# Decoder step on one core: how the attention deals out its eight PSUM banks

## The chip, the cores and the metric

The kernel runs as one program on one core of a Trainium2 chip. The metric is device time in microseconds (us) of one launch, lower is better. The core has a matmul engine (TensorE, PE in the profile, its weight loads PEld), VectorE (DVE), ScalarE (ACT), GpSimd (POOL), queues for DMA, a working memory (SBUF) and a small memory into which alone the matmul engine writes (PSUM). PSUM is used here as eight banks of 128 partitions by 512 fp32 values; a matmul's output lies in one bank, and VectorE or ScalarE copy it out (an eviction) before the bank is written again.

## The reference

One step of a decoder trunk with two layers, for 512 new prompt positions and 8 sequences with 4 new sample positions each, 544 columns in all, width 1024, fp32:

```python
for i in range(DEPTH):                     # 2 layers
    x = x + 0.5 * swiglu(rmsnorm(x, norm_ffn1[i]), w_ffn1_in[i], w_ffn1_out[i])
    h = rmsnorm(x, norm_mix[i])
    if i % 2 == 0:                         # dilated windows (128,1), (512,4), (2048,16)
        m = dilated_mixer(h, caches, w_qkv_a, w_out_a)
    else:                                  # chunked spatial gating
        m = chunk_gmlp(h, w_uv_b, ln_g, ln_b, w_s, b_s, w_out_b)
    x = x + m
    x = x + 0.5 * swiglu(rmsnorm(x, norm_ffn2[i]), w_ffn2_in[i], w_ffn2_out[i])
y = rmsnorm(x, norm_final)
```

In the mixer of layer 0, q, k and v of three groups (8 heads of 64 each) come from one projection. The prompt attends within itself, the sample positions attend to cached keys and values and to themselves; the three groups are merged by their softmax denominators and projected by `w_out_a`. The outputs are `y` and the new rows of the caches.

## The kernel before

**Products.** Weights stand still, the 544 columns of activations stream past in two halves of 272. Each fp32 matrix is split into a high and a low part (`split`, L234: ScalarE casts `wh`, VectorE subtracts `wl`), and a product runs three passes per 128 rows of the contraction (`passes`, L243, matmuls at L247): `wh` with the activations' high part, `wh` with their low part, `wl` with the high part. `plain` (L262) makes four results from one load of weights, two column blocks by two halves; each takes one bank `z`, accumulates 24 matmuls in it (8 blocks of 128 by three passes) and is then evicted by `take`, in the attention at a raised priority (`soon`, L134).

**The attention** (L752) works on pairs of heads, `hp` 0 to 3. `UNITS` (L31) is the program order of one pair, a prime marks work for the pair before:

```python
UNITS = "U1 AV' BV' b K1 B1 U2 rk1 K2 B2 A12 U0 E12 rk2 K0 B0 A0 D U3 E0 rk0 M v0 v1 U4 v2"
```

`U0` to `U4` are products that make q, k or v of a group; VectorE's eviction writes `qT`, `kT`, `vT` (L231). What begins with A, E, M, v and `rk` is the prompt's: scores (L864 and L895 into banks `sm`, masked by VectorE), exponentials, merge, and the values (L974): per block ScalarE scales the scores, PE transposes four blocks into a bank (L989, L1003), ScalarE copies them to `pt` (L991, L1005), and four matmuls add to the sum `ya` or `yb` (L994, L1008), each a bank held until the last block (L1010, L1011). What begins with b, B, K, D is the sample's, in banks `sb`: rows of q, k and v are transposed (L1027), q goes out to `q_rows` and comes back spread over the partitions as `qb` by DMA, POOL multiplies it with cached keys into `prod`, VectorE reduces that to scores `sc` (L1132); `decide` (L1149) makes the softmax; the values (L1179) add up in one bank `yo` from L1213 over L1216 to the copy at L1220, with POOL's products and VectorE's reductions (L1194) between.

At the end of the attention the output projection runs in two parts (L830, L836), each a contraction of 256, so that one result is six matmuls; its eviction adds to `x` (L410), which has been read back from `x_away`. The first part and all of the above lie between `heads(True)` (L781) and `heads(False)` (L833), that is, with `few` set.

**Banks and order.** `bank` (L108) deals out the banks by tags: tag "m" has four, "n" and "o" have two each. Outside the attention products rotate in "m" (`z`) and "n" (`z2`), small matmuls in "o". With `few` set, products take "n", the prompt's small matmuls "m", the sample's "o". A planner orders each engine's instructions when the program is built: by priority, which is program order unless raised, among what its own estimate of times says is ready, and a tile that finds none of its tag's buffers free waits for one. On the chip each engine then follows that order; semaphores make it wait for data and for banks. Only products of the first unit (before L781) run in the attention without `few`.

Of the kernel before, what the change touches and what calls it, by code (L numbers as in the profile page):

```python
# [94 lines left out]
class Ctx:  # L95
# [11 lines left out]

    def bank(self, kind):  # L108

        few = {"z": "n", "sm": "m", "sb": "o"}  # L110
        tag = (few if self.few else {"z": "m", "z2": "n", "sm": "o"})[kind]
        return self.pp.tile([P, 512], F32, tag=tag, name=f"ps_{kind}", bufs=4 if tag == "m" else 2)

    def heads(self, on):
# [1372 lines left out]
```

## Time and profile before

| | us |
|---|---|
| median of 3 runs | 2368.95 |
| lowest, highest | 2368.46, 2370.94 |
| the profiled execution | 2366.76 |
| its span, first to last instruction | 2365.0 |
| busy: PE, PEld | 2322.5, 2282.1 |
| busy: DVE, ACT, POOL | 1781.5, 1137.9, 117.5 |

The profile is of one execution. Busy time is the time in which an engine had an instruction in work; matmuls overlap each other in it. POOL works in the attention alone, from about 416 to 766 us of the span. A group of the profile is named by line, engine, operation and tiles, `ps_z` for a product's bank, `ps_sm` and `ps_sb` for those of the prompt's and the sample's small matmuls. "Idle before" is the time that the engine stood still ahead of an instruction, with what ended it. The granted clock is TensorE's, 1.00 at full speed.

### The profile page before, as it was taken

The numbers are of one execution on the slowest core, as the hardware profiler recorded it, in microseconds if no ns is written. First come the engines' busy times: TensorE is split into PE (matmuls) and PEld (weight loads), VectorE is DVE, ScalarE is ACT, GpSimd is POOL, SyncE is SP. The second block draws the span as 40 slices with busy tenths as digits, with TensorE's granted clock in tenths as the row PEclk, the third lists the DMA queues.
The fourth block names the chain that finished last, engine by engine and source line by source line (L and its number), as shares of the span: only waits on it lengthen the run. The fifth ranks groups of instructions, "written<-read, shape, count | busy, mean of one in ns | idle before, by whom it ended". The sixth has DMA issues, their size and how long they took to land.

```text
span 2365.0 us, 44134 instructions
## 1 busy us (share of the span) xinstructions
PE 2322.5 (98%) x18316; PEld 2282.1 (96%) x18316; DVE 1781.5 (75%) x3011; ACT 1137.9 (48%) x1879; POOL 117.5 (5%) x100
## 2 busy tenths in 40 slices
PE   8999999999999999999999999999999999999997
PEld 8999999989898999999999999999999999999997
DVE  8878585656656978768887858799977778878583
ACT  7444354444435734435644424666644536435253
POOL 0000000342332000000000000000000000000000
PEclk9999999999999999999999999999999999999999
DMA  4323235565554332323232323334433322223231
GB/s 148 107 90 108 75 124 161 137 179 163 146 159 118 119 108 90 108 77 120 72 107 86 112 72 118 99 129 143 138 112 115 101 90 90 90 90 123 74 117 39
DMA packets 308000, 263.40 MB, mean 111 GB/s; under 512 B 7352, under 2 KB 303384, under 8 KB 307800
## 3 DMA queue, kind: packets, MB, share of 16 engines
q1 hardware_dynamic: 284104, 242.88, 33.0%
q10 hardware_dynamic: 23696, 17.70, 2.6%
q8 instruction: 144, 2.36, 0.4%
q14 instruction: 56, 0.46, 0.1%
HBM read 243.78 MB, written 16.78 MB: 110 GB/s over the span
## 4 chain that ended last, share of the span: by engine, by line
PE 89%; DMA 4%; DVE 2%; POOL 1%; issue 1%; ACT 1%; ACTq 0%; POOLq 0%; DVEq 0%; SPq 0%
PE ps_z L247 84%; POOL prod L231 1%; DMA other<-in_cache_kv_w_dram 1%; DMA q_rows<-sn 1%; DMA qb<-q_rows 1%; PE ps_sm L1361 1%; PE ps_sm L1290 0%; ACT wh L238 0%; DVE wl L231 0%; PE ps_sm L864 0%; PE ps_sb L1213 0%; PE ps_sb L1117 0%; PE ps_sm L1363 0%; PE ps_z L685 0%; DVE s L231 0%
## 5 line engine op out<-in xcount | busy, mean ns | idle before, releaser
L247 PE MATMUL ps_z<-xbh,wh 128*128 128x272 f32 x2164 | 629.6, 294 | 6.9 <-DVE x L410 2.3
L247 PE MATMUL ps_z<-xbl,wh 128*128 128x272 f32 x2164 | 625.3, 290 | 0.0
L238 ACT CAST wh<-raw 128x1024 fp32r<-128x1024 f32 (+3 forms) x404 | 355.3, 881 | 553.2 <-PE ps_z L247 528.6
L247 PE MATMUL ps_z<-xbh,wl 128*128 128x272 f32 x2164 | 620.4, 290 | 0.0
L247 PE MATMUL ps_z<-abh,wl 128*128 128x272 f32 x1792 | 516.3, 290 | 0.0
L247 PE MATMUL ps_z<-abl,wh 128*128 128x272 f32 x1792 | 513.8, 288 | 0.0
L247 PE MATMUL ps_z<-abh,wh 128*128 128x272 f32 x1792 | 512.3, 288 | 0.3 <-ACT abh L204 0.3
L247 PE MATMUL ps_z<-th,wh 128*128 128x272 f32 x1648 | 477.1, 290 | 5.1 <-DVE f L375 2.7
L247 PE MATMUL ps_z<-th,wl 128*128 128x272 f32 x1648 | 477.6, 290 | 0.0
L247 PE MATMUL ps_z<-tl,wh 128*128 128x272 f32 x1648 | 476.3, 290 | 0.4 <-DVE tl L231 0.4
L231 DVE TENSOR_TENSOR wl<-raw,wh 128x1024 fp32r<-128x1024 f32 (+3 forms) x404 | 411.2, 1021 | 54.4 <-ACT wh L238 52.5
L247 PEld LDWEIGHTS ps_z<-xbh,wh 128*128 128x128 f32 x2164 | 407.2, 189 | 15.7 <-issue 4.1
L247 PEld LDWEIGHTS ps_z<-xbl,wh 128*128 128x128 f32 x2164 | 409.7, 189 | 1.9 <-issue 0.8
L247 PEld LDWEIGHTS ps_z<-xbh,wl 128*128 128x128 f32 x2164 | 406.5, 189 | 2.2 <-issue 1.5
L238 ACT CAST wh<-s 128x1024 fp32r<-128x1024 f32 x206 | 216.4, 1050 | 257.1 <-PE ps_z L247 251.6
L247 PEld LDWEIGHTS ps_z<-abl,wh 128*128 128x128 f32 x1792 | 337.4, 189 | 0.1
L247 PEld LDWEIGHTS ps_z<-abh,wl 128*128 128x128 f32 x1792 | 336.6, 188 | 0.2
L247 PEld LDWEIGHTS ps_z<-abh,wh 128*128 128x128 f32 x1792 | 335.3, 188 | 0.6 <-ACT abh L204 0.5
L247 PEld LDWEIGHTS ps_z<-th,wh 128*128 128x128 f32 x1648 | 311.3, 189 | 6.4 <-DVE f L375 3.2
L247 PEld LDWEIGHTS ps_z<-tl,wh 128*128 128x128 f32 x1648 | 311.1, 189 | 0.9 <-DVE tl L231 0.6
L247 PEld LDWEIGHTS ps_z<-th,wl 128*128 128x128 f32 x1648 | 311.2, 189 | 0.3
L231 DVE TENSOR_TENSOR wl<-s,wh 128x1024 fp32r<-128x1024 f32 x206 | 251.3, 1220 | 33.2 <-ACT wh L238 33.0
(275 smaller groups left out, 2427.4 us busy)
## 6 DMA issues: line engine op xcount, KB each, us to landing
raw<-in_w_ffn_in_dram SPq DMA_DIRECT2D x88, 1024.0 KB, 5.1
raw<-in_w_ffn_out_dram SPq DMA_DIRECT2D x32, 1024.0 KB, 5.2
raw<-in_w_uv_b_dram SPq DMA_DIRECT2D x24, 1024.0 KB, 5.3
raw<-in_w_qkv_a_dram SPq DMA_DIRECT2D x36, 512.0 KB, 5.2
other<-in_cache_kv_w_dram SPq DMA_DIRECT2D x28, 512.0 KB, 4.8
raw<-in_w_ffn_out_dram SPq DMA_DIRECT2D x16, 768.0 KB, 4.4
raw<-in_w_out_b_dram SPq DMA_DIRECT2D x16, 768.0 KB, 4.4
other<-in_cache_kv_w_dram SPq DMA_DIRECT2D x28, 256.0 KB, 3.5
```

Source lines behind the costliest of these rows:

```text
L231: eng.tensor_tensor(out, a, b, op=op)
L238: g.nc.scalar.copy(t[0], a)
L247: g.nc.tensor.matmul(z, a, b, start=(first and s == 0), stop=(last and s == 2), skip_group_check=True)
L1361: nc.tensor.matmul(pm[:, n * P:(n + 1) * P], vn[:, n, iss], wst[:, gq], start=True, stop=True)
```

## The change

With `few` set, a product now takes its bank from the tags "n" and "o" in turn, two banks each, so four in rotation. The small matmuls of prompt (`sm`) and sample (`sb`) both take tag "m", four banks together, where they had four and two. Outside the attention nothing changes. `turn` is set to False by `heads` and was used before only in `banks`, which no product between L781 and L833 calls.

```diff
     def bank(self, kind):
 
-        few = {"z": "n", "sm": "m", "sb": "o"}
-        tag = (few if self.few else {"z": "m", "z2": "n", "sm": "o"})[kind]
+        if self.few:
+
+            self.turn = not self.turn if kind == "z" else self.turn
+            tag = "m" if kind != "z" else "no"[self.turn]
+        else:
+            tag = {"z": "m", "z2": "n", "sm": "o"}[kind]
         return self.pp.tile([P, 512], F32, tag=tag, name=f"ps_{kind}", bufs=4 if tag == "m" else 2)
```

## The prediction

> **What bounds the kernel now.** I read the page first: span, busy time of the engines, costliest groups.
>
> ```profile
> span 2365.0 us, 44134 instructions
> ...
> L247 PE MATMUL ps_z<-xbh,wh 128*128 128x272 f32 x2164 | 629.6, 294 | 6.9 <-DVE x L410 2.3
> ```
>
> The products (L247, `ps_z`) are the big groups and they hardly wait: 6.9 us of idle time in front of this one. The matmul engine sets the time, and only its gaps can be had. The change acts on the attention alone, so I cut that stage into windows (columns: PE, PEld, DVE, ACT, POOL busy, granted clock, DMA).
>
> ```profile
> 416.00:476.00 60.00, 58.83 (x447) 53.96 (x446) 38.72 (x100) 24.96 (x66) 20.77 (x12) 1.00 0.53 141
> ...
> 716.00:766.00 50.00, 47.06 (x350) 42.57 (x349) 36.24 (x74) 25.94 (x72) 13.93 (x16) 0.90 0.41 121
> sum 350.00, PE 335.78 PEld 309.52 DVE 221.22 ACT 148.58 POOL 117.27; mean PE 55.96 PEld 51.59 DVE 36.87 ACT 24.76 POOL 19.54
> ```
>
> ```profile
> 830.00:890.00 60.00, 60.00 (x479) 60.00 (x478) 42.64 (x66) 22.70 (x29) 0.00 (x0) 1.00 0.33 106
> ```
>
> Of 350 us PE is busy 335.78: 14.2 us idle, 0.6% of the span, is the most that any order of the same work could win here, apart from the half-clock stretches below. The window of the FFN in the second fence has no gap at all. What ends the gaps is in the waits of PE in the stage (what waits, for whom, us in total, times, longest):
>
> ```profile
> PE ps_sm L864 <- DVE kT L231: 3.6, 2, 2.9
> PE ps_z L247 <- DVE x L410: 2.3, 3, 1.6
> PE ps_sb L1027 <- DVE kT L231: 2.1, 2, 1.1
> PE ps_z L247 <- DVE kT L231: 2.1, 2, 1.8
> PE ps_sb L1213 <- DVE ssum L1209: 1.3, 1, 1.3
> PE ps_sb L1113 <- DMA other<-in_cache_kv_w_dram: 0.8, 1, 0.8
> PE ps_z L247 <- DVE qT L231: 0.8, 1, 0.8
> ```
>
> Two kinds must be kept apart. A product that waits for DVE's write of `kT`, `qT` or `x` reads none of these: it waits for the bank which that eviction empties. These **bank waits** are 2.3 + 2.1 + 0.8 = 5.2 us. A small matmul that waits for `kT` (L864, the scores; L1027, a transpose) or for `ssum` (L1213) reads that very tile: these **data waits** are 3.6 + 2.1 + 1.3 = 7.0 us. The longest of each, DVE's rows ahead of PE's (the timeline: start, us, what, in brackets the idle time before and what ended it):
>
> ```profile
> 594.45 1.22 DVE L1132 TENSOR_REDUCE sc<-prod 128x16 f32<-128x1024 f32 x1 [3.38 <-POOL prod L231]
> 595.58 0.68 DVE L1011 TENSOR_TENSOR y<-y,ps_sm 128x512 f32<-128x512 f32 x1
> 596.78 1.22 DVE L1132 TENSOR_REDUCE sc<-prod 128x16 f32<-128x1024 f32 x1 [0.53 <-POOL prod L231]
> 597.92 0.62 DVE L231 TENSOR_TENSOR kT<-ps_z,rstd 128x272 f32<-128x272 f32 x1
> ```
>
> ```profile
> 596.13 0.71 PE L895 MATMUL ps_sm<-kT,qT 64*128 64x128 f32 x6
> 598.60 0.39 PE L247 MATMUL ps_z<-xbh,wh 128*128 128x272 f32 x1 [1.75 <-DVE kT L231]
> ```
>
> ```profile
> 532.00 0.43 DVE L231 TENSOR_TENSOR kT<-ps_z,rstd 128x272 f32<-128x272 f32 x1
> ```
>
> ```profile
> 528.23 0.28 PE L247 MATMUL ps_z<-xbh,wh 128*128 128x272 f32 x1
> 528.35 0.29 PE L247 MATMUL ps_z<-xbl,wh 128*128 128x272 f32 x1
> ...
> 528.98 0.60 PE L963 MATMUL ps_sm<-cst,kT 128*128 128x128 f32 x4
> 532.48 0.49 PE L864 MATMUL ps_sm<-kT,qT 64*128 64x128 f32 x4 [2.91 <-DVE kT L231]
> ```
>
> The reader is to see the same cause twice: DVE takes its queue in order, the eviction of `kT` stands behind reductions of the sample's scores (L1132), and these wait for POOL. PE then stands still, once for the bank and once for the data.
>
> **The change part by part.** No instruction is added or removed; banks are dealt out differently, and the planner orders PE's work anew by its own estimate of when banks come free.
>
> *Products: two banks become four.* Products start 0.12 to 0.13 us apart (528.23, 528.35), so a half of 24 matmuls takes 3.0 us. With two banks PE may run one half ahead of the eviction; with four, three. Two more halves are 6.0 us of cover against a longest bank wait of 1.8 us; in the output projection a half has six matmuls, 0.75 us, so two more cover 1.5 of the 1.6 us. The 5.2 us of bank waits therefore go almost whole, as waits.
>
> What is late next is the data. DVE still works its queue at POOL's pace: before the wait at 598.60 it idles 3.38 and 0.53 us for POOL, and four banks hurry neither. PE runs ahead, then meets the next small matmul whose tile DVE has not written. Below, nothing is given back (5.2 us won), above, everything (0 won). I take half, 2.6 us, since bank and data waits are of like size and stand beside each other in the same stretches. The planner may also put the next unit's products into the hole between the last eviction and the scores (528.98 to 532.48), which two banks forbade: from 0 to the 7.0 us of data waits; I take 0.5 us, since what made that wait long is POOL's lateness, and the planner that set this order did not see it.
>
> *Small matmuls: four banks and two become four in all.* This adds waits. Who holds banks long is seen in one head's values:
>
> ```profile
> 572.58 0.44 PE L994 MATMUL ps_sm<-pt,spare 128*64 128x128 f32 x4
> ...
> 574.82 1.44 PE L1213 MATMUL ps_sb<-ssum,cache 128*128 128x64 f32 x11
> ...
> 583.09 0.66 PE L1008 MATMUL ps_sm<-pt,spare 128*64 128x128 f32 x8
> ```
>
> ```profile
> 582.65 0.59 ACT L1010 COPY y<-ps_sm 128x512 f32<-128x512 f32 x1 [1.38 <-PE ps_sm L994]
> 584.38 1.07 ACT L1005 COPY pt<-ps_sm 128x512 f32<-128x512 f32 x2 [1.14 <-PE ps_sm L1003]
> 585.62 0.43 ACT L1220 COPY y<-ps_sb 64x32 f32<-64x32 f32 x2 [0.16 <-PE ps_sb L1216]
> ```
>
> The prompt's first sum `ya` is written from 572.58 and copied out at 582.65, ten microseconds; the sample's sum `yo` from 574.82 to 585.62, eleven; the second sum `yb` from 583.09 until DVE reads it at 595.58 (L1011 above), twelve. So of four shared banks two are bound for most of it, and two are left for the transposes and for the next head's sample rows, where four were left before, three of the prompt's and one of the sample's. Two suffice to alternate, since a step is four transposes (L989 or L1003), a copy by ACT of about 0.53 us (1.07 for two) and four matmuls. A transposing matmul that finds no bank stops everything behind it on PE, products included, until ACT's copy lands.
>
> The price: below zero is possible, as longer runs of one kind save switches; a first product behind small ones comes 0.23 us before the next (598.60 to 598.83 in the same timeline) and not 0.125, so a switch costs about 0.1 us. Above, all eight steps of four heads wait for a copy: 32 × 0.53 = 17 us. Three heads have the next head's products to lay between, and there a bank short of one is a different order and some more switches: 0.1 us × 8 × 3, at half, 1.2 us. The last head has almost no products left, but its eight steps were alternating already; I put nothing there. I take 1 us in all, near the lower end, by the switch, because the rows show ACT waiting for PE at every copy (1.38, 1.14), and not the other way round.
>
> ```profile
> 598.83 0.29 PE L247 MATMUL ps_z<-xbl,wh 128*128 128x272 f32 x1
> ```
>
> *The clock.* Three stretches of the stage ran at half the granted clock:
>
> ```profile
> 492.08:495.49 3.41, 3.41 (x24) 2.75 (x20) 3.31 (x5) 1.65 (x4) 2.36 (x4) 0.50 0.89 259
> 533.05:536.46 3.41, 3.41 (x16) 3.41 (x17) 3.29 (x8) 0.22 (x1) 0.00 (x0) 0.50 0.75 217
> 737.85:748.08 10.23, 10.23 (x48) 9.68 (x46) 9.15 (x10) 5.32 (x14) 5.85 (x7) 0.50 0.82 232
> ```
>
> 17.05 us at half clock cost up to 8.5 us. The second follows the data wait at 532.48, the others stretches of small matmuls. Since the longest data wait stays, I expect them to stay: 0, with bounds of one stretch fewer or more, 3.41/2 = 1.7 us each way. [...]
>
> **The sum.** −2.6 − 0.5 + 1 + 0 = −2.1 us. The profiled execution spans 2365.0 us and took 2366.76 us, 2.2 us under the median of 2368.95 us; I apply the difference to the median: 2368.95 − 2.1 ≈ **2366.8 us**. A change under 0.2%, 4.7 us, can't be told from none here.
>
> **The rivals.**
> - *PE really runs ahead* (faster): the bank waits go whole (−5.2), the new order closes half of the data waits (−3.5), and the stretch behind 532.48 keeps its clock (−1.7), against +1 for the shared banks: −9.4, 2359.5 us. For it: PE is the bound, and each gap stands beside products that only a bank held back. Against it: DVE's idle time for POOL is unchanged.
> - *Small matmuls wait for banks* (slower): the place is the values of a head, above all of the last, where no product covers. If two sums and `yo` hold three banks and transposes are left with one, each step waits for ACT's copy. The last head alone: 8 × 0.53 = 4.2; four steps each of the other three: 12 × 0.53 = 6.4; one more half-clock stretch 1.7; less the 2.6 won: +9.7, 2378.7 us. It decides the sign from about seven exposed copies on (7 × 0.53 = 3.7, against 3.1 won), and is slower by over 0.2% from about fifteen. For it: the three sums are held 10 to 12 us each. Against it: `yo` and `yb` overlap for 2.5 us only (583.09 to 585.62).
> [...]
> - *It does not do what it says*: the planner orders as before and PE stalls a few us later for the same DVE rows; 2369 us.
>
> **How the numbers follow.** Forecast, about 2 us won: 0.40. Does nothing: 0.07. Faster, 2359.5: 0.31. Shared banks, slower, 2378.7: 0.19. Clock: 0.03. Those within 0.2% give 0.47; faster 0.31; slower 0.22, the clock's rival counted as slower. The likeliest alone lies in 2364.2 to 2368.9. The range reaches past the faster case, to 2358, and into the slower one, to 2377, where the price of 17 us above makes its end uncertain: left out are about half of the slower case and the far end of the faster, some 0.15.
>
> **What would show it.** In PE's waits of the attention the rows `ps_z L247 <- DVE x, kT, qT` shrink from 5.2 to under 1.5 us. L864 and L1027 waiting for `kT` keep or grow beyond 5.7 us: then half is given back. If `ps_sm` or `ps_sb` rows waiting for ACT copies (`pt`, `sn`, `kt`) come to microseconds, the shared banks bite, first of all after 737. PE's idle time in 416 to 766 should be 11 to 13 us in place of 14.2, and the half-clock time about 17 us. The prediction is wrong if the new order of PE, which no row of this profile can show, moves the sample's transposes (L1027) by microseconds: they start the chain over DMA and POOL on which DVE waits.

## The result, and the profile after

| | before | after |
|---|---|---|
| median of 3 runs, us | 2368.95 | 2410.85 |
| lowest, highest | 2368.46, 2370.94 | 2408.77, 2411.03 |
| span of the profiled execution, us | 2365.0 | 2406.9 |

The ratio is 1.0175, 95% interval 1.0157 to 1.0192: 41.9 us slower. The forecast was 2366.8 us, and 2410.85 lies far above the range's end of 2377. (In the lines of after, a line number is 4 higher than in before.)

From the page of after: the span, the granted clock in 40 slices, and the group of the products.

```profile
span 2406.9 us, 44133 instructions
...
PEclk9999999999995999999999999999999999999999
...
L251 PE MATMUL ps_z<-xbh,wh 128*128 128x272 f32 x2164 | 627.4, 293 | 8.4 <-DVE x L414 7.0
```

The products are what they were, 2164 of 293 ns in this group. One slice of the clock, at the end of the attention, has fallen to 5. To see how much the stage lost, both kernels are cut at the end of their last small matmul, so that the windows hold the same work. First before, then after (columns as in the windows of the prediction):

```profile
416.00:760.20 344.20, 330.31 (x2625) 304.88 (x2624) 217.08 (x472) 145.95 (x390) 117.27 (x96) 0.98 0.54 151
```

```profile
416.00:801.50 385.50, 345.12 (x2626) 314.21 (x2626) 226.77 (x473) 146.03 (x388) 116.07 (x96) 0.92 0.49 135
```

2625 and 2626 matmuls, 96 instructions of POOL in each: the same work takes 385.5 in place of 344.2 us, 41.3 us more, which is nearly all of the 41.9 us by which the two spans differ. PE's idle time grew from 13.9 to 40.4 us (26.5), its busy time by 14.8 us at a mean clock of 0.92 for 0.98. Where the idle time lies, the windows of after by stage show:

```profile
416.00:476.00 60.00, 57.64 (x436) 53.25 (x436) 34.63 (x83) 20.78 (x53) 15.41 (x8) 1.00 0.50 134
...
656.00:716.00 60.00, 59.67 (x476) 55.13 (x475) 36.94 (x81) 26.72 (x73) 13.27 (x16) 1.00 0.30 89
716.00:766.00 50.00, 26.01 (x148) 20.81 (x148) 26.55 (x72) 13.20 (x48) 19.95 (x14) 0.63 0.49 139
```

Over the five windows up to 716 PE is busy 291.9 us where it was 288.7. Then it is busy 26.01 of 50 us where it was 47.06, at a clock of 0.63 where it was 0.90. The waits of PE in the stage name what it waits for there:

```profile
PE ps_sb L1117 <- DMA cache<-in_cache_kv_w_dram: 15.4, 2, 14.3
PE ps_z L251 <- DVE x L414: 7.0, 2, 6.6
PE ps_sb L1096 <- ACT sn L1033: 6.4, 3, 5.2
PE ps_sm L952 <- DVE wm L948: 3.4, 3, 1.8
PE ps_sb L1178 <- DVE dn L1176: 2.6, 1, 2.6
```

The product's waits for `kT` and `qT` are gone; the longest wait is now a transpose of cached keys that waits 14.3 us for its DMA. That transfer was not slow, it was issued at 736.26 and PE went on 4.3 us later, at 740.59 (the medians of its kind in after are 4.6 us for 256 KB and 6.0 us for 512 KB); it was late. What it hangs on shows in the chain that ended last in after (start, us, what):

```profile
715.92 1.93 PE ps_sb L1217 x16
717.85 0.23 PE ps_sb L1031 x2
...
718.85 3.14 DMA q_rows<-sn
722.00 3.86 DMA qb<-q_rows
...
726.02 2.34 POOL prod L235
728.38 5.37 DMA cache<-in_cache_kv_w_dram
...
733.89 2.35 POOL prod L235
736.26 4.19 DMA cache<-in_cache_kv_w_dram
...
740.59 1.94 PE ps_sb L1117 x8
```

From the row transposes (L1031) the chain goes out over DMA to `q_rows`, back as `qb`, over POOL and two loads of the caches to PE's transposes. In before the same view has no piece of `q_rows` or `qb` in the last head (from 670 us on). POOL's timeline, first after, then before:

```profile
726.02 2.34 POOL L235 TENSOR_TENSOR prod<-cache,qb 128x1024 f32<-128x1024 f32 x1 [32.40 <-DMA qb<-q_rows]
```

```profile
677.38 2.38 POOL L231 TENSOR_TENSOR prod<-cache,qb 128x1024 f32<-128x1024 f32 x1 [15.35 <-DMA qb<-q_rows]
...
699.42 5.04 POOL L231 TENSOR_TENSOR prod<-other,qb 128x512 f32<-128x512 f32 x4 [12.60 <-DMA qb<-q_rows]
```

POOL stood idle for 32.40 us of the last head for `qb`, the sample's q rows on their way over DMA. That alone is little more than before, where it waited 15.35 and 12.60 us for them, 28.0 together. What has moved is the start: POOL's first product with `qb` begins at 726.02 in place of 677.38, 48.6 us later. It is POOL's products, among others, that free the buffers into which more of the caches is loaded (SP's waits from 700 to 760 have 7.7 us for POOL's `prod`). In after `qb` is loaded from 722.00 on, as the chain shows; in SP's timeline of before it was loaded at 673.61 and 695.68:

```profile
673.61 0.63 SPq L1084 DMA_DIRECT2D qb<-q_rows  x1
...
695.68 0.63 SPq L1084 DMA_DIRECT2D qb<-q_rows  x1
```

So the sample's chain starts late in the last head. It does in the others too. PE around the start of the sample's rows of the second pair of heads, first before, then after:

```profile
486.16 0.43 PE L1213 MATMUL ps_sb<-ssum,cache 128*128 128x64 f32 x2
486.52 0.44 PE L994 MATMUL ps_sm<-pt,spare 128*64 128x128 f32 x4
486.89 1.53 PE L989 MATMUL ps_sm<-cst,S 128*128 128x128 f32 x12
488.26 1.67 PE L1213 MATMUL ps_sb<-ssum,cache 128*128 128x64 f32 x14
489.77 0.27 PE L1027 MATMUL ps_sb<-cst,qT 128*32 128x128 f32 x1
```

```profile
519.60 1.15 PE L1012 MATMUL ps_sm<-pt,spare 128*64 128x128 f32 x16
520.68 2.00 PE L1217 MATMUL ps_sb<-ssum,cache 128*128 128x64 f32 x16
522.51 0.27 PE L1031 MATMUL ps_sb<-cst,qT 128*32 128x128 f32 x1
```

Before, the sample's sum `yo` (L1213) starts beside the first matmuls of the prompt's first sum (L994), and the row transposes (L1027) follow 3.6 us later. After, `yo` starts at 520.68, behind sixteen matmuls of the prompt's *second* sum (L1012), and the transposes at 522.51, 33 us later than before. That is the order of the program: in `UNITS` the prompt's values AV' stand ahead of the sample's BV', and these ahead of `b` and K1. With a tag of its own the sample could take a bank while the prompt's values waited for theirs. With one tag, banks are handed out in program order, and a sample tile is behind every prompt tile that stands ahead of it.

It holds the other way round too: a prompt tile is behind every sample tile ahead of it. In `UNITS` the sample's softmax D stands ahead of the prompt's merge M. First before, then after:

```profile
464.39 0.74 PE L921 MATMUL ps_sm<-m,csta 128*128 128x16 f32 x6
...
469.44 0.28 PE L1174 MATMUL ps_sb<-dn,csta 128*128 128x8 f32 x2
```

```profile
477.33 0.28 PE L1178 MATMUL ps_sb<-dn,csta 128*128 128x8 f32 x2
...
477.61 0.96 PE L925 MATMUL ps_sm<-m,csta 128*128 128x16 f32 x8
```

Before, the merge (L921) begins five microseconds ahead of the softmax's last product (L1174); after, directly behind it (L925, L1178), 13 us later. The first transposes of the prompt's values then come at 502.96 in place of 481.77 (L993, L989). So of the 33 us by which the row transposes are late, 21 lie ahead of the values, and about 12 come from standing behind them. I call this the **one line**: two chains that went side by side become one.

### The profile page after: what moved, and what is told of

It reads as the page before. It is cut to its first block, busy times and chain, and to the rows that moved or that the text cites. A ratio compares the mean times of both kernels' runs of the same rounds, so it can differ in the third digit from the quotient of the medians.

```text
span 2406.9 us, 44133 instructions
## 1 busy us (share of the span) xinstructions
PE 2336.4 (97%) x18316; PEld 2291.1 (95%) x18316; DVE 1790.3 (74%) x3011; ACT 1138.4 (47%) x1879; POOL 116.3 (5%) x100
## 4 chain that ended last, share of the span: by engine, by line
PE 89%; DVE 4%; DMA 3%; ACT 2%; issue 1%; POOL 1%; ACTq 0%; SPq 0%; POOLq 0%; DVEq 0%
PE ps_z L251 82%; POOL prod L235 1%; PE ps_sm L1365 1%; DVE wl L235 1%; PE ps_sm L868 1%; DMA q_rows<-sn 1%; DMA cache<-in_cache_kv_w_dram 1%; ACT wh L242 1%; DVE spare L1198 1%; DMA qb<-q_rows 1%; PE ps_sm L1294 0%; DVE s L235 0%; PE ps_sb L1121 0%; PE ps_sm L993 0%; PE ps_sb L1217 0%
```

## The experiments

The ratios are against before, run in the same job; each edit is shown against after unless it says otherwise, and `...` stands for lines left out. The expectations weigh the one line against its rivals: too few banks for the small matmuls, the sample's rows being late in themselves, a last head left without cover, and the half clock.

**One part of the change alone.** The small matmuls share tag "m"; the products keep two banks, and "o" stays unused.

```diff
-            self.turn = not self.turn if kind == "z" else self.turn
-            tag = "m" if kind != "z" else "no"[self.turn]
+            tag = "m" if kind != "z" else "n"
```

> Products keep two banks, prompt and sample share four, two banks lie idle. Line (theory: one tag hands out its banks in program order, so the sample's rows stand behind the prompt's values of the head before, start their DMA and POOL chain 30 to 50 us late, and the last head has no products left to cover it): as slow as the change, 2400 to 2415 us, the second group's q rows of the last head near 715 us as with the change (669 before). Products ahead (theory: four product banks let products overtake the small matmuls): 2366 to 2372 us, rows near 669. Number (theory: four small banks are too few in place of six): slow as well, 2400 to 2415.

2405.74 against 2366.09 us, ratio 1.0165 (1.0150 to 1.0180), +39.65 us, in the range that both the one line and too few banks had given. All of the loss that can be told from the noise is in the sharing. The profile repeats after's: the stage's window and the waits of PE.

```profile
416.00:793.20 377.20, 344.65 (x2619) 311.54 (x2618) 225.68 (x472) 145.73 (x387) 117.46 (x96) 0.93 0.50 138
```

```profile
PE ps_sb L1115 <- DMA cache<-in_cache_kv_w_dram: 12.6, 2, 12.1
PE ps_z L249 <- DVE x L412: 6.6, 1, 6.6
...
PE ps_z L249 <- DVE kT L233: 2.7, 3, 1.2
```

With two banks the bank wait for `kT` is back (2.7 us), and it costs nothing that can be measured: the ratio's interval overlaps that of after.

**One line with as many banks as before.** Prompt and sample share six banks, the number that the two of them had in before, products have two.

```diff
-            self.turn = not self.turn if kind == "z" else self.turn
-            tag = "m" if kind != "z" else "no"[self.turn]
+            tag = "n" if kind == "z" else "q"
...
-            tag = {"z": "m", "z2": "n", "sm": "o"}[kind]
+            tag = {"z": "q", "z2": "q", "sm": "n"}[kind]
-        return self.pp.tile([P, 512], F32, tag=tag, name=f"ps_{kind}", bufs=4 if tag == "m" else 2)
+        return self.pp.tile([P, 512], F32, tag=tag, name=f"ps_{kind}", bufs=6 if tag == "q" else 2)
```

> Products have two banks, prompt and sample share six (outside the attention products share those six and small matmuls have two, which should move the stages outside by less than 3 us). Line: slow, 2385 to 2410 us, rows of the last head after 695 us, although the small matmuls have six banks. Number: 2364 to 2374. Products ahead: 2364 to 2374.

2391.83 us, ratio 1.0102 (1.0085 to 1.0119), +25.7 us: in the range of the one line, and outside that of the two rivals. Between L781 and L833 this differs from before in one thing only, that the six banks are one tag. So the one line alone, with no bank fewer, costs 25.7 us; the two banks fewer of share_only add 13.9 us. The marks of the line are there: the merge (L923) at 476.66, directly behind the sample's softmax (L1176 at 476.38), and the first `qb` of the last head loaded at 710.18, 36.6 us later than in before. Behind the attention it is as before: span less the end of the small matmuls is 2392.8 − 788.0 = 1604.8 us, before 2365.0 − 760.2 = 1604.8.

**Three ways to give the sample a line of its own beside more product banks.** Products turn over "n" and "o", the sample takes "o" too, the prompt keeps "m":

```diff
-            tag = "m" if kind != "z" else "no"[self.turn]
+            tag = {"sm": "m", "sb": "o"}.get(kind) or "no"[self.turn]
```

> Products turn over four banks as in the change, the sample shares two of these, the prompt keeps four of its own. Line: the prompt no longer stands ahead of the sample, 2362 to 2372 us, rows of the last head within 10 us of 669. Products ahead: slow, 2390 or more. Number: about 2370, since the small matmuls have six again.

2397.56 us, ratio 1.0130 (1.0115 to 1.0146): a miss of the one line as I had put it, since prompt and sample are apart here, and in the range that was given to products running ahead. The first `qb` of the last head is loaded at 697.70, 24 us later than in before, where at most 10 were expected. The sample now shares a tag with the products; that the two hold each other up in it is a guess. PE has 6.8 us of idle time in a stretch where before had 1.2, as the first window shows, and the waits there are for data of DVE and ACT.

```profile
416.00:476.00 60.00, 53.22 (x355) 48.43 (x353) 36.45 (x92) 21.37 (x61) 21.44 (x14) 0.86 0.50 134
```

Four banks for products, two for the prompt, two for the sample:

```diff
-            self.turn = not self.turn if kind == "z" else self.turn
-            tag = "m" if kind != "z" else "no"[self.turn]
+            tag = {"z": "m", "sm": "n", "sb": "o"}[kind]
```

> Products have four banks, prompt two, sample two: four small banks as in the change, but two lines. Line: 2362 to 2380 us, with some loss from the prompt's two banks, rows of the last head within 15 us of 669. Number: slow, 2395 or more. Products ahead: slow, 2395 or more.

2422.3 us, ratio 1.0233 (1.0218 to 1.0249), the slowest of all, and a second miss; both rivals had 2395 or more. It is no longer the sample that is late: the first `qb` of the last head is loaded at 677.84, 4 us later than in before. The longest waits are others:

```profile
PE ps_z L249 <- DVE x L412: 9.5, 3, 5.4
PE ps_sm L950 <- DVE wm L946: 5.5, 3, 2.7
PE ps_sm L897 <- DVE m L900: 3.3, 3, 1.5
PE ps_sm L965 <- ACT spare L967: 3.1, 1, 3.1
PE ps_sm L1010 <- ACT pt L1007: 2.7, 4, 0.7
PE ps_sm L996 <- ACT pt L993: 2.4, 4, 0.7
```

Of the small matmuls' waits the long ones are the prompt's. By the program one of its two banks holds a sum, and the transposes have one left. The waits for ACT's copies `pt`, which the prediction had put at the centre of its slower rival, are here, and together they are 5.1 us. These waits do not add up to the 56.2 us that this kernel loses.

Three banks for products, three for the prompt, two for the sample:

```diff
+        self.count = getattr(self, "count", -1) + (kind == "z")
+        turn = "mmmp"[self.count % 4]
...
-            self.turn = not self.turn if kind == "z" else self.turn
-            tag = "m" if kind != "z" else "no"[self.turn]
+            tag = "nnp"[self.count % 3] if kind == "z" else {"sm": "m", "sb": "o"}[kind]
...
-            tag = {"z": "m", "z2": "n", "sm": "o"}[kind]
+            tag = {"z": turn, "z2": "n", "sm": "o"}[kind]
-        return self.pp.tile([P, 512], F32, tag=tag, name=f"ps_{kind}", bufs=4 if tag == "m" else 2)
+        return self.pp.tile([P, 512], F32, tag=tag, name=f"ps_{kind}", bufs={"m": 3, "p": 1}.get(tag, 2))
```

> Products three banks in turn, prompt three, sample two, each a line of its own. Line: the small matmuls keep their order, 2360 to 2372 us; of the 5.2 us of product waits for banks at most 1 us is left and up to 5 us are won. Number (five small banks in place of six): 2375 to 2390. Products ahead (more product banks let products overtake): 2380 or more.

2386.6 us, ratio 1.0074 (1.0053 to 1.0095), a third miss, in the ranges of both rivals. Its stage has before's idle time and before's clock, and yet is longer:

```profile
416.00:774.80 358.80, 345.26 (x2634) 310.36 (x2632) 218.47 (x472) 145.79 (x390) 116.17 (x96) 0.98 0.53 146
```

13.5 us idle (before 13.9), but 345.26 us busy where before had 330.31. Products and small matmuls change places more often in it, 106 times for 81 between 416 and 716, counted in the trace; at the 0.1 us per switch of the prediction this is 2.5 us, or 5 with both ways counted, and does not explain 15. Counted from start to start without the idle time, over the whole stage and both ways, the changes of place take 40.0 us (236 of them) where before had 29.4 (182), the time among small matmuls grew by 4.2 us, and that among products not at all. So most of the 15 us lies at the changes; why one costs more stays open. Behind the attention, too, it takes 5.8 us more than before (2385.4 − 774.8 = 1610.6), where its products rotate in other tags.

The three together say that a tag of its own for the sample is not enough. Each of them also gives the products more banks, and that this costs time in them is not excluded.

**The sample's rows earlier, in one line.** K1, which transposes the rows, is moved ahead of the values in `UNITS`, in after, in the kernel with six shared banks, and in before.

```diff
-UNITS = "U1 AV' BV' b K1 B1 U2 rk1 K2 B2 A12 U0 E12 rk2 K0 B0 A0 D U3 E0 rk0 M v0 v1 U4 v2"
+UNITS = "U1 b K1 AV' BV' B1 U2 rk1 K2 B2 A12 U0 E12 rk2 K0 B0 A0 D U3 E0 rk0 M v0 v1 U4 v2"
```

> The change, with the sample's first rows (b K1) ahead of the values of the head before (AV' BV') in the program order. Line (one tag hands out its banks in program order; what stands late in the line starts its DMA and POOL chain late, and the last head then has no products left to cover it): the first q rows of the last head go out 10 to 25 us earlier than with the change (718.8 us there) and the time falls to 2380 to 2400 us. Number (four small banks are too few, whatever their order): no better than 2405. Cover alone (products run ahead, wherever the rows stand): no better than 2405.

> One line of six banks for prompt and sample, with the sample's first rows ahead of the values. Line: 10 to 20 us under the same without the move (2391.8 us), 2370 to 2383. If the lateness of these rows is not the cause: 2388 to 2395.

> The kernel before with its banks, the sample's first rows (b K1) ahead of the values of the head before. Line: a little of what the move won with a shared line, the rows of the last head 3 to 12 us earlier than 670.0, 2362 to 2370 us. If the move is neutral where the sample has its own banks: 2366 to 2371.

In after the move does to the order what the one line says: in SP's timeline the first `qb` of the last head is loaded at 695.72 in place of 722.00.

```profile
695.72 0.63 SPq L1088 DMA_DIRECT2D qb<-q_rows  x1
...
719.88 0.63 SPq L1088 DMA_DIRECT2D qb<-q_rows  x1
```

But the time is 2405.4 us, ratio 1.0156 (1.0139 to 1.0174), not to be told from after: a miss of the one line, in the range of too few banks and of cover alone. Only the first of the two loads came much earlier; the second, at 719.88 (726.13 in after), is that of K2, which stands behind the values still. And K1 too still stands behind the merge and all that is ahead of it in the line: in the second pair of heads its row transposes come at 502.87, just ahead of the values (503.10), where before had them at 489.77. With six banks the same move gives 2383.15 us, 1.0063 (1.0046 to 1.0079), 8.7 us less than share_six, a little under the 10 to 20 expected: where the line has banks to spare, its order counts. In before it gives 2375.35 us, 1.0032 (1.0019 to 1.0045), slower than either expectation, so the move itself is no gain.

**The sample's rows late, with the old banks.** In before, K1, B1, K2 and B2 are moved behind A12 and U0. The edit is shown against before.

```diff
-UNITS = "U1 AV' BV' b K1 B1 U2 rk1 K2 B2 A12 U0 E12 rk2 K0 B0 A0 D U3 E0 rk0 M v0 v1 U4 v2"
+UNITS = "U1 AV' BV' b U2 rk1 A12 U0 K1 B1 K2 B2 E12 rk2 K0 B0 A0 D U3 E0 rk0 M v0 v1 U4 v2"
```

> The kernel before with its banks, the sample's K1 B1 K2 B2 moved behind A12 U0 in the program order: both rows of the last head go out some 12 to 25 us later than the first of them did (670.0). Late rows (the start of the sample's chain is what costs): 2375 to 2390 us, with PE waiting for POOL, DMA or the sample's banks after 716. If lateness of the rows costs nothing as long as the banks are apart: 2362 to 2372.

2379.62 us, ratio 1.0047 (1.0032 to 1.0062), +11.9 us, as expected of late rows, and the rows of the last head leave for DMA at 703.8 us, against 670.0 in before and 718.8 in after. Lateness of that chain alone makes a part of the loss, not the whole.

**Which heads pay.** The change's banks only while `hp` is 0 to 2 in the loop of the units (before's from 3 on), and the other way round.

```diff
+            if not (self.hp < 3):
+                tag = {"z": "n", "sm": "m", "sb": "o"}[kind]
...
+            g.hp = hp
```

> The change's banks for the units of heads 0 to 2, those of before from the fourth pass of the unit list on (head 3 and the values of head 2 in it, and the output projection). Tail (theory: in heads 0 to 2 the small matmuls fall behind and the products run ahead, at no loss; the price is paid once, where the products have run out and the small matmuls of the last head stand alone, idle and at half clock): between both, 2372 to 2390 us, by how much of the lag is carried into head 3: 160 to 260 small matmuls left when the last q, k, v product is evicted (364 with the change, 152 before). Each head (theory: every head loses about 10 us): 2393 to 2400.

> The banks of before for the first three passes of the unit list, those of the change from the fourth on. Tail: the products have no lead when the last head begins, so less than with the change: 2372 to 2390 us, with 160 to 260 small matmuls left. Each head: 2374 to 2382 with no more small matmuls left than before (152).

2386.31 us, 1.0080 (1.0063 to 1.0096), and 2386.54 us, 1.0083 (1.0065 to 1.0101): +17.7 and +17.9 us, together 35.5 of the 41.9. Both times lie in the range of the tail theory and outside that of each head. The stretch from the last eviction of a q, k or v product to the last small matmul, in before and then in early_only:

```profile
725.80:760.20 34.40, 31.79 (x233) 28.15 (x233) 26.90 (x51) 17.90 (x48) 13.93 (x16) 0.85 0.50 145
```

```profile
715.80:778.00 62.20, 51.83 (x359) 44.26 (x357) 42.80 (x98) 29.22 (x86) 19.99 (x21) 0.78 0.46 131
```

Counted in the traces, 282 small matmuls are left in this stretch in early_only, against 152 in before, 364 in after and 160 in late_only. So in early_only the small matmuls fall behind in the heads that have products to lay between, and the products run ahead, by 10 us; the time is lost at the end, after the q, k and v products have run out. In late_only hardly more is left than in before, but the same stretch takes 48.9 us (727.0 to 775.9) in place of 34.4.

**A last head left without cover.** One theory of after was that products, freed by four banks, run ahead, and that the last head's small matmuls are then alone at the end. Two products of the last head are held back on PE, U0 behind the row transposes of K2 and U3 behind that of K0, each being the last ahead of it in `UNITS`; then the same in all heads, and in all heads with two product banks.

```diff
-                    do[t](h)
+                    with g.tc.issue_after(g.row_ins.ins) if h == 3 and t in ("U0", "U3") else ExitStack():
+                        do[t](h)
...
-            nc.tensor.transpose(ps[:32, i * P:(i + 1) * P], tl[nm, gi][:, TP:], g.ident)
+            g.row_ins = nc.tensor.transpose(ps[:32, i * P:(i + 1) * P], tl[nm, gi][:, TP:], g.ident)
```

> The change with its banks, but in head 3 alone the products of U0 and U3 are queued on PE behind the sample's second rows (K2), so they can't run ahead. Tail (the loss is paid where the products have run out before the last head's small matmuls): the last q, k, v product comes later and fewer small matmuls are left then (120 to 200 in place of 364), PE idles less behind it, 2370 to 2392 us. Shared line (prompt and sample in one line cost the time wherever the products stand): 2400 or more, the idle time of the tail moved ahead of U0.

> The same in every head. Tail: no better than hold_last by more than 5 us, since heads 0 to 2 lost nothing, 2368 to 2392. Each head: 8 to 15 us better than hold_last. Shared line: 2400 or more.

> As hold_all, with two banks for products and two idle ones. If four product banks win what the prediction took (2 to 5 us of bank waits): 2 to 5 us slower than hold_all. If they win nothing: within 2 us of it.

hold_last: 2409.42 us, 1.0170 (1.0154 to 1.0185). The cover is there, and the time is not:

```profile
656.00:716.00 60.00, 45.20 (x309) 37.41 (x307) 31.04 (x68) 24.07 (x66) 14.03 (x16) 0.77 0.33 95
716.00:766.00 50.00, 45.37 (x326) 40.98 (x326) 30.86 (x86) 15.80 (x54) 16.84 (x10) 0.97 0.40 119
```

In 716 to 766 PE is now busy 45.37 us where after had 26.01, at a clock of 0.97 for 0.63; the hole has moved to 656 to 716, 45.20 where after had 59.67; the longest wait there, 9.9 us, is the prompt's merge for DVE's `wm`. The small matmuls end at 799.0, in after at 801.5. Wherever the products stand, the line takes its time: the theory that cover is all that is missing fell, and the shared line's 2400 or more came true. hold_all gives 2412.58 us, 1.0191 (1.0171 to 1.0212), hold_two 2416.38, 1.0195 (1.0177 to 1.0213). The 3.8 us between them are of the size expected if four product banks win, but the intervals overlap, and share_only with two banks was not slower than after; whether four banks win anything is not settled.

**The half clock.** In share_only, eight matmuls of 512 columns that nothing reads are put into the idle banks at each of two places of the last head, ready when its `qb` has landed.

```diff
+                    if h == 3 and t in ("K1", "K2"):
+                        fill = g.pp.tile([P, 512], F32, tag="o", name="ps_fill", bufs=2)
...
+                        for j in range(8):
+                            nc.tensor.matmul(fill, g.ident, q, start=(j == 0), stop=(j == 7))
```

> Products two banks, prompt and sample share four, and 16 extra matmuls of 512 columns into the idle banks, ready when the last head's q comes back from q_rows; nothing reads their result. If the half clock of the tail costs time: half-clock time after 716 falls from 54.6 us to under 35 and the end comes 4 to 12 us earlier than without them, 2394 to 2402 us. If the tail is bound by the chain over DMA, POOL and ScalarE alone: 2404 to 2420, later by up to the 14 us that these matmuls take.

2420.5 us, 1.0227 (1.0204 to 1.0249), 14.8 us more than share_only and just past the 2404 to 2420 given for a tail bound by the chain. The half-clock stretch at the end shrinks from 54.6 to 47.8 us only, where under 35 was expected. The clock of 716 to 766 rises from 0.60 in share_only to 0.79, but the added matmuls take 13.3 us of PE (in its timeline, 6.17 and 7.13 us), ahead of small ones:

```profile
716.00:766.00 50.00, 38.85 (x171) 25.18 (x169) 22.82 (x65) 12.53 (x45) 18.61 (x12) 0.79 0.39 115
```

What the half clock costs by itself is not settled by this.

No version that was tried is faster than before. Among them are two that only change the program order and leave the banks as they were (before_keys_first, keys_late, 6.7 and 11.9 us slower). So part of each loss may be that of any new order; the 25.7 us of share_six are more than either.

## Why the prediction was wrong, point by point

**"Products: two banks become four"** was right in what happens: the waits for `kT` and `qT` went. `x` rose from 2.3 to 7.0 us by a single wait of 6.6 at the output projection, which share_only has with two banks. The idle time of 416 to 716 fell from 11.3 to 8.1 us, 3.1 us, which is by chance the −2.6 − 0.5 of the forecast; but share_only, with two product banks, has 6.2 us there (300 less the five windows' busy time), so the four banks are not what won it. "What is late next is the data" failed: the scores and transposes wait no longer for `kT` (0.4 us in after, 5.7 in before), presumably because they run so late that their data have long been there.

**"Small matmuls: four banks and two become four in all"** is the step that failed. It was put at +1 us, with 17 us as the upper end, and share_only measures it alone: +39.65 us. The 1 us counted switches, and the 17 us PE standing before a transpose until ACT's copy lands; that wait (`ps_sm` for `pt`) is 0.5 us in after. "Three of the prompt's and one of the sample's" were counted as four alike, and what was lost was for the greater part not their number but that the sample's bank could be had *past* the prompt's, and the prompt's past the sample's. share_six shows it: 25.7 us with no bank fewer, against 13.9 that the two banks fewer add. Nothing bounded the effect of a new order on the chain over DMA and POOL; the last sentence of the prediction named it as what would make it wrong ("if the new order of PE … moves the sample's transposes (L1027) by microseconds"), and they moved by 33 us. The last head, where "I put nothing", is where the time is lost. A condition that could be named should have had a price and a chance: the 48.6 us by which POOL's first product with `qb` begins later in the last head show of which size it was.

**"The clock"**, put at 0, came with the idle time. One stretch of after, the window of its half clock:

```profile
728.20:789.60 61.40, 31.82 (x123) 25.03 (x124) 34.99 (x69) 20.88 (x67) 25.46 (x24) 0.50 0.47 131
```

61.4 us, where before had 17.05 in its whole attention. It holds 31.82 us of busy time, so that at full clock at most about half of that, 15.9 us, would be had back (an estimate: products in it start 0.22 to 0.23 us apart, at 767.68, 767.90 and 768.13, and 0.12 to 0.13 at full clock), against at most 8.5 before. What lowered the clock is not shown. It does not hang on the products' four banks: share_only, with two product banks and not four, has a clock of 0.60 in 716 to 766 where after has 0.63. PE's 14.3 us wait for the cached keys, up to 740.59, had begun 1.9 us before the stretch; but in before the clock fell three times, and the longest wait of PE in its attention is 2.91 us.

**The rivals.** "Small matmuls wait for banks" (0.19) had the right sign and the right culprit, the shared banks, but neither mechanism (exposed copies) nor price (+9.7 for +41.9). Its place ("above all of the last" head) is where the time is lost, but the small matmuls fall behind in the heads before it (early_only loses as much as late_only). "PE really runs ahead" is what products did, and it won nothing that can be measured: the small matmuls end last. The clock had a chance of 0.03, as a rival of its own with more half-clock stretches; no run shows a source for it. What the runs show is more half-clock time, 61.4 us in after's one stretch and 54.6 us at the end of share_only, and that does not make the clock the cause.

**What is shown and what is not.** Shown: the sharing makes the loss (share_only), the one line makes most of that with no bank missing (share_six), and it does so with the products held back, too (hold_last, hold_all). The small matmuls fall behind in the heads before the last as well as in it (early_only, late_only). That banks are granted past each other in before and in program order in after is read from PE's order, and agrees with what keys_first moved in that order; the time it moved only with six banks. Not settled: the half clock's own share and what lowers the clock, how much any new order costs, and why the three kernels with prompt and sample apart are slower, apart_332 without more idle time.

## What to carry to other kernels

Here two chains that drew on one pool of buffers, handed out in program order, became one chain; it counted more what stands ahead of a chain's first tile (25.7 us in share_six, with no bank fewer) than how many buffers there are (13.9 us more in share_only, with two banks fewer). Price a change of pools at the start of the chain with the longest way over other engines and DMA, and not only at the waits of the busiest engine. To tell order from shortage, merge the pools at the same total number of buffers.

## What was not expected of the hardware

In after TensorE stayed at half clock (0.50 from 728.20 to 789.60) for 61.4 us in one piece while it worked 31.82 us of them, in 123 matmul records, most of them small matmuls. In before the three stretches were over after 3.41, 3.41 and 10.23 us, with PE at work throughout. What ended them was not shown. In apart_332 about the same 2630 matmuls took 15 us more busy time than in before (345.26 for 330.31) at the same mean clock of 0.98, only in another order.
